# One large product a step ahead of the scores, value products of a pair in two runs, norm rows on VectorE: one change to a hybrid attention and mLSTM step

## The chip, the cores and the metric

The kernel runs on 1 core of one Trainium2 chip. The metric is device time in microseconds (us) from start to end of one execution. Engines are called by the profile's short names: PE (TensorE, matrix products; PEld its weight loads), ACT (ScalarE), DVE (VectorE), POOL (GpSimd) and SP (SyncE, which issues DMAs). Each engine takes its instructions strictly in the order in which the program lists them for it; a wait for another engine holds all that stands behind it.

## The reference, cut to what matters

One layer of a hybrid backbone: 128 context tokens and 1024 latent tokens of width 1024, so 9 blocks of 128 tokens (block 0 is the context). Grouped-query attention (8 query heads of 64, 2 key heads) and a bidirectional mLSTM run side by side; the output projection joins them, and a SwiGLU follows. All is float32.

```python
aq = apply_rope(rmsnorm(aq.reshape(B, T, N_Q_HEADS, HEAD_DIM), q_norm_w), *rope)
s = jnp.einsum('bqhgd,bkhd->bhgqk', qi, k).astype(F32) * ATTN_SCALE
p = jax.nn.softmax(s, axis=-1).astype(v.dtype)
o = jnp.einsum('bhgqk,bkhd->bqhgd', p, v)
...
mix = jnp.concatenate([attn_o, hm], axis=-1) @ w_out        # hm: the mLSTM's part
x = x + g1 * mix
h2 = rmsnorm(x, norm2_w) * (1 + sc2) + sh2
x = x + g2 * swiglu(h2, w_gu, w_down)
```

Each latent block of 128 queries has 1152 keys (1024 latent, 128 context), so a head's scores are 128 x 1152.

## The kernel before

Modulation, input projection, keys and the mLSTM come first; the gate, up and down products of the SwiGLU fill the second half of the span. Between them lies the stage that the change touches: attention over the 8 latent blocks, with the remaining query products, the output projection and the second norm woven in.

**Steps.** The stage is a Python loop over steps. Step n belongs to head n of 64 (block 1 + n // 8, head n % 8). Before the change a step writes, in this order: the scores of head n + 2 on PE (`head_scores`, six matmuls at L1110 into one of two score buffers, which the exponential of head n must have left); filler work on PE; in odd steps the value products of a pair of heads (18 matmuls at L1053, for the two heads n - 3 and n - 2); on DVE and ACT the normalised probabilities of head n as a float16 pair (`ph` at L1509, `pl` at L1517), each turned by a DMA transpose; the maximum (L1114) and the exponential (L1118) of head n + 1; the sums of the value products of the step before (ACT L1058 and L1059 into `ol`, POOL L1061); then filler work on ACT and DVE. One `ph` a step makes it the clock by which steps are counted.

**Fillers.** `Filler` holds tasks as generators. Each piece of a task names its engine, a cost, a lag in steps behind the piece before it, the PSUM banks it needs and a condition. `run` writes the pieces whose lag, bank and condition allow it as long as the engine's credit is above zero; the credit grows each step by PE 3.5, ACT 1.9, DVE 2.0 and is capped at one and a half of that. The pieces with lag 0 are written after the others. Names such as `turned` or `rope` are stamped with the step in which a piece was written. The tasks:

- `q_task(b)`, blocks 3 to 8: a query product in two halves (12 matmuls each, L1287 to L1289), copied to `q_rest` (ACT L726). The blocks go in pairs (3, 4), (5, 6), (7, 8); with the second of a pair comes its rope: a square on ACT (L663, into a scratch tile that the rope's products reuse), a sum and a small chain on DVE (L666; L125 to L131), then seven operations on POOL (L669, four of L680, L686, L687).
- `turn_task(b)`: four PE transposes of a block's roped queries (L114, `q_rest`), copies and splits into `qT`. It may start two steps after the rope is stamped, and for block 3 not ahead of step 9.
- `hm_task(b)`: the mLSTM's rows of a block are transposed and split (`ring`), and the output projection's lower half runs as two products of 12 matmuls (`out_block`, L1142 to L1144); the gated sum goes to the residual rows (DVE L1133, POOL L1136).
- `mix_task(b)`: the same for the attention's half when a block's heads are done (`kst`), then the second norm: sum of squares (ACT L1425), a reciprocal root (DVE L1189 to L1196), rows scaled by it (`norm_rows`, ACT L1432, twice 512 columns into two tiles `y`), eight PE transposes into two banks, scale and shift (ACT L1451, DVE L1453), and a float16 split (ACT L1461, POOL L135).
- `w_task`, `first_piece`: loads and splits of the out weights and of the first gate weights.

The last block's norm is done by `norm2`, beside the first gate products (L1180 to L1182).

Of the kernel before, what the change touches and what calls it, by code (L numbers as in the profile page):

```python
# [45 lines left out]
def hybrid_step(ctx: ExitStack, tc: tile.TileContext, I: dict, O: dict):  # L46
# [998 lines left out]
    def value_products(b, j, nk, kv, rhs):  # L1045
        if j == 0:
            oT[b] = new_oT(b)
        po = po2[:, n_po[0] % 2 * 256 : n_po[0] % 2 * 256 + 256]
        n_po[0] += 1
        for n in range(nk):  # L1050
            v = vs[:, NB if nk == 1 else n, kv].rearrange("p t d -> p (t d)")
            for t in range(2):
                mm(po, v, rhs(t, n), start=(n == 0 and t == 0), stop=(n == nk - 1 and t == 1))  # L1053
        return b, j, po
# [92 lines left out]
    def norm2(b, new=None):  # L1147
# [6 lines left out]
        for half in range(2):  # L1154
            y = fp.tile([P, 512], F32, name=nm("y"), tag="y", bufs=2)
            act(y, x1[b][:, half * 512 : (half + 1) * 512], AF.Copy, scale=rs[b])
            pss.append(y)
            yield 0.1
# [73 lines left out]
    class Filler:  # L1232

        def __init__(self, **per_step):
            self.per_step, self.credit = per_step, dict.fromkeys(per_step, 0.0)
            self.tasks, self.step, self.banks = [], 0, 2
# [9 lines left out]
        def run(self, engine, behind=False):  # L1246
            order = sorted((t for t in self.tasks if t[1][0] == engine), key=lambda t: t[1][1])
            for task in order:
                while task[1] is not None:
# [3 lines left out]
                    if not behind and self.credit.get(engine, 1.0) <= 0.0 or ready is not None and not ready():  # L1253
                        break
                    if engine in self.credit:
# [12 lines left out]
    fl = Filler(PE=3.5, ACT=1.9, DVE=2.0)  # L1268
# [8 lines left out]
    def q_task(b):  # L1277
# [18 lines left out]
        yield "ACT", 1.1, 0, 0, lambda: b - 2 < CB or ("rope", b - 2) in at  # L1296
# [88 lines left out]
    def mix_task(b):  # L1385
# [15 lines left out]
        yield "ACT", 1.35, 1, 0, lambda: b == 0 or ("turned", b - 1) in at  # L1401
# [26 lines left out]
    def norm_rows(b):  # L1428
        ys = []
        for half in range(2):  # L1430
            y = fp.tile([P, 512], F32, name=nm("y"), tag="y", bufs=2)
            act(y, x1[b][:, half * 512 : (half + 1) * 512], AF.Copy, scale=rs[b])  # L1432
            ys.append(y)
        return ys
# [55 lines left out]
    def step(n):  # L1490
# [3 lines left out]
        if n + 2 < len(heads):  # L1494
            head_scores(n + 2)
        fl.run("PE")
# [3 lines left out]
        elif n % 2 == 1 and (n - 3) // 2 in pairs:  # L1500
            m = (n - 3) // 2
            two = pairs.pop(m)
            now = [value_products(heads[2 * m][0], m % 4, NB, m % 4 // 2, lambda t, i: two[t][:, :, i, :])]
# [105 lines left out]
    pairs, late = {}, []  # L1609
    pieces = [Piece(0, lambda: wp.tile([P, 1024], F32, name=nm("braw"), tag="raw", bufs=2), ("whi", "wlo"))]  # L1610
    pieces += [Piece(f) for f in range(1, NF)]
    with tc.manual_schedule(engines=ENGINES):
# [22 lines left out]
        while n < len(heads) + 4 or fl.tasks:  # L1635
# [263 lines left out]
```

## Time and profile before

| | us |
|---|---|
| median of 3 runs | 1646.91 (1644.01 to 1648.23) |
| the profiled execution's own time | 1645.31 |
| its span, first to last instruction | 1643.5 |
| first score product starts | 435.1 |
| first gate product starts | 837.45 |

A row of the profile that shows an instruction has its start, its length, the engine, the line, the operation and what it writes and reads; brackets give the engine's idle time ahead of it and what ended it. A row for a group of instructions has the count, the busy time in us, the mean in ns, and the idle time ahead of the group with its main releasers. Tile names appear without their numbers. A PE row's length includes the pipeline, so the distance of starts is the better measure of a run of matmuls. The chain of work that ended last covers only the last part of this stage; the stage is therefore read by windows and waits.

### The profile page before, as it was taken

To read this page: it belongs to the slowest core of one execution; us is meant where nothing else is said; L and a number is where in the kernel's file an instruction comes from. 1 tells how busy PE (TensorE), PEld (TensorE's weight loads), DVE (VectorE), ACT (ScalarE), POOL (GpSimd) and SP (SyncE) were. 2 spreads that over 40 slices of the span, in tenths; PEclk is the share of its full clock that TensorE was granted. 3 is DMA by queue.
4 is the path that set the end of the run, shared out by engine and by line. 5 is a ranking of instruction groups with operands and counts; after the bars stand their busy time and mean duration, and the time that the engine had idled before them with its cause. 6 is when DMAs were issued, how large, how long until landed. Compare 5 with 4: busy or idle time off the path is not lost.

```text
span 1643.5 us, 22904 instructions
## 1 busy us (share of the span) xinstructions
PE 1489.5 (91%) x8651; PEld 921.1 (56%) x8651; DVE 902.0 (55%) x2160; ACT 732.4 (45%) x1428; POOL 251.1 (15%) x272
## 2 busy tenths in 40 slices
PE   5899999898596799877689989999999999999995
PEld 2755666575454677655455555456664466655542
DVE  3844355849765777877645456333353333442278
ACT  3744343345465666778655666003340032422023
POOL 0411021303224522333320000000000000000001
PEclk8899999999598899999799999999999999999998
DMA  9345462301285789556357553421104310120213
GB/s 353 114 142 150 93 144 62 73 1 19 60 174 99 149 190 193 101 102 127 72 180 252 184 194 100 140 93 52 52 27 141 115 52 28 50 77 14 83 59 116
DMA packets 281685, 181.83 MB, mean 111 GB/s; under 512 B 167302, under 2 KB 253782, under 8 KB 281574
## 3 DMA queue, kind: packets, MB, share of 16 engines
q1 hardware_dynamic: 280150, 177.96, 41.6%
q10 hardware_dynamic: 1424, 2.40, 0.4%
q8 instruction: 68, 1.11, 0.3%
q14 instruction: 43, 0.35, 0.1%
HBM read 122.71 MB, written 19.29 MB: 86 GB/s over the span
## 4 chain that ended last, share of the span: by engine, by line
PE 37%; DMA 5%; DVE 4%; ACT 4%; issue 1%; POOL 0%; ACTq 0%; SPq 0%; DVEq 0%; POOLq 0%
PE mm L1180 8%; PE mm L1182 8%; PE mm L1181 8%; PE mm L1751 4%; PE mm L1752 4%; PE mm L1753 4%; DMA wd_d<-wdt 3%; DMA wdt<-in_w_down_dram 2%; DVE x L1136 1%; ACT wdt L1546 1%; DVE wdt L1552 1%; ACT wdt L1551 1%; DVE t L1135 1%; ACT jk L1576 0%; ACT jk L1837 0%
## 5 line engine op out<-in xcount | busy, mean ns | idle before, releaser
L1180 PE MATMUL mm<-h,wpair 128*128 128x384 f16 x1056 | 345.0, 327 | 1.5 <-DVE fl L1453 1.5
L1181 PE MATMUL mm<-h,wpair 128*128 128x384 f16 x1056 | 345.0, 327 | 0.0
L1182 PE MATMUL mm<-h,wpair 128*128 128x384 f16 x1056 | 344.7, 327 | 0.0
L1714 DVE SCALAR_TENSOR_TENSOR tn<-tn,mm 128x384 f32<-128x384 f32 x66 | 36.4, 552 | 217.5 <-PE mm L1182 139.6
L1751 PE MATMUL mm<-wd,hl 128*128 128x512 f16 x396 | 149.9, 379 | 0.0
L1752 PE MATMUL mm<-wd,hl 128*128 128x512 f16 x396 | 149.9, 379 | 0.0
L1753 PE MATMUL mm<-wd,hl 128*128 128x512 f16 x396 | 149.6, 379 | 0.0
L1180 PEld LDWEIGHTS <-wpair 128*128 128x128 f16 x1056 | 105.4, 100 | 67.3 <-issue 0.7
L1182 PEld LDWEIGHTS <-wpair 128*128 128x128 f16 x1056 | 103.5, 98 | 68.7 <-issue 0.7
L1181 PEld LDWEIGHTS <-wpair 128*128 128x128 f16 x1056 | 103.5, 98 | 68.7 <-issue 2.3
L1110 PE MATMUL S<-kst,qT 128*128 128x512 f32 (+1 forms) x384 | 97.3, 394 | 47.9 <-ACT pr L1118 46.0
L499 PE MATMUL wi<-ipair,hT 128*128 128x384 f16 (+2 forms) x384 | 124.7, 325 | 2.8 <-ACT ipair L216 2.8
L1840 POOL TENSOR_TENSOR x<-x,fw 128x512 f32<-128x512 f32 x9 | 11.5, 1274 | 756.7 <-ACT jk L1837 756.7
L501 PE MATMUL wi<-ipair,hT 128*128 128x384 f16 (+2 forms) x384 | 124.4, 325 | 0.4 <-POOL hT L135 0.4
L500 PE MATMUL wi<-ipair,hT 128*128 128x384 f16 (+2 forms) x384 | 124.7, 325 | 0.0
L1717 ACT ACTIVATE jk<-tn 128x384 bf16<-128x384 f32 x66 | 34.4, 521 | 196.8 <-DVE tn L1715 145.1
L1576 ACT ACTIVATE jk<-braw 128x1024 bf16<-128x1024 f32 x44 | 45.9, 1044 | 152.9 <-DVE x L1136 152.1
L1517 DVE SCALAR_TENSOR_TENSOR pl<-pr,st,ph 128x1152 f16<-128x1152 f32 x64 | 95.1, 1486 | 31.9 <-ACT ph L1509 29.0
L1509 ACT ACTIVATE ph<-pr,st 128x1152 f16<-128x1152 f32 x64 | 80.3, 1254 | 68.0 <-issue 59.6
L1110 PEld LDWEIGHTS S<-kst,qT 128*128 128x128 f32 x384 | 69.9, 208 | 72.2 <-ACT pr L1118 58.6
L1114 DVE TENSOR_REDUCE st<-S 128x1 f32<-128x1152 f32 x64 | 86.7, 1355 | 39.9 <-PE S L1110 39.4
L1135 DVE SCALAR_TENSOR_TENSOR t<-mm,gm,gl 128x512 f32<-128x512 f32 x64 | 47.7, 745 | 81.3 <-PE mm L1753 81.3
(427 smaller groups left out, 2854.5 us busy)
## 6 DMA issues: line engine op xcount, KB each, us to landing
wd<-wd_d SPq DMA_DIRECT2D x58, 512.0 KB
braw<-in_w_gu_dram SPq DMA_DIRECT2D x44, 512.0 KB
a4s<-in_w_ada_dram SPq DMA_DIRECT2D x32, 512.0 KB
wdt<-in_w_down_dram SPq DMA_DIRECT2D x22, 512.0 KB
wd_d<-wdt SPq DMA_DIRECT2D x22, 512.0 KB
aw<-in_w_ada_dram SPq DMA_DIRECT2D x16, 512.0 KB
x<-in_x_sample_dram SPq DMA_DIRECT2D x16, 512.0 KB
iraw<-in_w_in_dram SPq DMA_DIRECT2D x32, 256.0 KB
```

The lines of the kernel that those rows point to most:

```text
L499: mm(ps[:, :n], ah, wh[:, k % 2, c0 : c0 + n], start=(k == 0), stop=False)
L500: mm(ps[:, :n], ah, wl[:, k % 2, c0 : c0 + n], start=False, stop=False)
L501: mm(ps[:, :n], al, wh[:, k % 2, c0 : c0 + n], start=False, stop=(k == KD - 1))
L1110: mm(S[:, lo:hi], qTs[b][:, h, :], kst[kv][:, t, lo:hi], start=(t == 0), stop=(t == 1))
L1114: dve.tensor_reduce(out=stat[n][:, 0:1], in_=score[n], axis=AX.X, op=ALU.max, negate=True)
L1180: mm(ps, wh[:, k, :], th[:, k, :], start=(k == 0), stop=False)
L1181: mm(ps, wh[:, k, :], tl[:, k, :], start=False, stop=False)
L1182: mm(ps, wl[:, k, :], th[:, k, :], start=False, stop=(k == KD - 1))
L1517: dve.scalar_tensor_tensor(out=pl, in0=pr, scalar=st[:, 3:4], in1=ph, op0=ALU.mult, op1=ALU.subtract)
L1751: mm(ps, ah, w[:, k, 0], start=(j + k == 0), stop=False)
L1752: mm(ps, ah, w[:, k, 1], start=False, stop=False)
L1753: mm(ps, al, w[:, k, 0], start=False, stop=(j + k == g["nf"] - 1))
```

## The change

Three things are done.

- **The order of a step on PE.** The filler pieces of a step now stand ahead of its scores. A piece of cost above 2.0 (a half of a query product or an out-projection product) is written at most once a step, and PE's credit grows by 3.3. The value products of a pair are cut in two: key blocks 0 to 4 (10 matmuls) behind the scores of the odd step, key blocks 5 to 8 (8 matmuls) at the head of the next step. Their sums are written a step later, and the loop has one step more at its end.
- **The rope.** The square of a pair's rope is written not as soon as the rope of the pair before it is stamped, but at least 3 steps after that.
- **The norm's rows.** `norm_rows` is one DVE operation of 128 x 1024 into one tile in place of two ACT operations of 128 x 512 into two, in the eight mixes and in `norm2`.

```diff
-    def value_products(b, j, nk, kv, rhs):
-        if j == 0:
+    def value_products(b, j, nk, kv, rhs, po=None, part=(0, NB)):
+        if j == 0 and po is None:
             oT[b] = new_oT(b)
-        po = po2[:, n_po[0] % 2 * 256 : n_po[0] % 2 * 256 + 256]
-        n_po[0] += 1
-        for n in range(nk):
+        if po is None:
+            po = po2[:, n_po[0] % 2 * 256 : n_po[0] % 2 * 256 + 256]
+            n_po[0] += 1
+        for n in range(nk)[slice(*part)]:
...
+                    if engine == "PE" and cost > 2.0:
+                        if self.big == self.step:
+                            break
+                        self.big = self.step
...
-    fl = Filler(PE=3.5, ACT=1.9, DVE=2.0)
+    fl = Filler(PE=3.3, ACT=1.9, DVE=2.0)
...
-        yield "ACT", 1.1, 0, 0, lambda: b - 2 < CB or ("rope", b - 2) in at
+        yield "ACT", 1.1, 0, 0, lambda: b - 2 < CB or since(("rope", b - 2), 3)
...
-        yield "ACT", 1.35, 1, 0, lambda: b == 0 or ("turned", b - 1) in at
+        yield "DVE", 0.75, 1, 0, lambda: b == 0 or ("turned", b - 1) in at
         ys = norm_rows(b)
...
     def norm_rows(b):
-        ys = []
-        for half in range(2):
-            y = fp.tile([P, 512], F32, name=nm("y"), tag="y", bufs=2)
-            act(y, x1[b][:, half * 512 : (half + 1) * 512], AF.Copy, scale=rs[b])
-            ys.append(y)
-        return ys
+        y = fp.tile([P, D], F32, name=nm("y"), tag="y", bufs=1)
+        dve.tensor_scalar(out=y, in0=x1[b], scalar1=rs[b], scalar2=None, op0=ALU.mult)
+        return [y[:, 0:512], y[:, 512:1024]]
...
-        if n + 2 < len(heads):
-            head_scores(n + 2)
-        fl.run("PE")
         now = []
         if n < 2:
             now = [value_products(*first_values[2 * n + i]) for i in range(2)]
-        elif n % 2 == 1 and (n - 3) // 2 in pairs:
+        elif n % 2 == 0 and half:
+            args, po = half.pop()
+            now = [value_products(*args, po, (5, NB))]
+        fl.run("PE")
+        if n + 2 < len(heads):
+            head_scores(n + 2)
+        if n % 2 == 1 and (n - 3) // 2 in pairs:
             m = (n - 3) // 2
             two = pairs.pop(m)
-            now = [value_products(heads[2 * m][0], m % 4, NB, m % 4 // 2, lambda t, i: two[t][:, :, i, :])]
+            args = (heads[2 * m][0], m % 4, NB, m % 4 // 2, lambda t, i: two[t][:, :, i, :])
+            half.append((args, value_products(*args, None, (0, 5))[2]))
...
-        while n < len(heads) + 4 or fl.tasks:
+        while n < len(heads) + 5 or fl.tasks:
```

In the changed program the lines from there on have other numbers: the scores' matmuls are L1111, the value products L1054, `ph` L1513, the query products L1290 to L1292, the out-projection products L1143 to L1145.

What this does to the order of instructions is shown at three places, with one row for each run of like matmuls. The first is PE in steps 8 and 9, where block 3's queries are transposed (`mm<-ident,q_rest`). Before, from the scores of head 10 on (`S2`, the score buffers; `ipair` and `hT2` make a query product, here both halves of block 7's):

```order
L1110 MATMUL S2_4796<-kst0_4270,qT_938_4856 128x128 x2
L1287 MATMUL mm_1015_5301<-ipair_790_4255,hT2_293 128x512
L1110 MATMUL S2_4796<-kst0_4270,qT_938_4856 128x512 x4
L114 MATMUL mm_1024_5342<-ident_79,q_rest_4274 128x128 x4
L1287 MATMUL mm_1015_5301<-ipair_792_4262,hT2_293 128x512
```

Now, from the value products ahead of the scores of head 10 on (the query product is block 6's):

```order
L1054 MATMUL po2_4797<-phT_978_5081,vs_4789 128x256
L1290 MATMUL mm_1013_5268<-ipair_790_4255,hT2_293 128x512
L1111 MATMUL S2_4796<-kst0_4270,qT_938_4856 128x128 x2
L114 MATMUL mm_1020_5301<-ident_79,q_rest_4274 128x128 x4
L1290 MATMUL mm_1013_5268<-ipair_792_4262,hT2_293 128x512
L1111 MATMUL S2_4796<-kst0_4270,qT_938_4856 128x512 x4
```

The transposes stood behind the scores of head 11 and stand ahead of them now, in the same step 9. The stamp of the first pair's rope moves from step 6 to step 7.

The second place is ACT around the square of the second pair's rope (`nr0`, L663). Before, from `ph` of head 7 on:

```order
L1509 ACTIVATE ph_1009_5277<-pr_999_5209,st_998_5207 128x1152
L1118 ACTIVATE pr_1012_5283,st_1011_5281<-S2_4796,st_1011_5281 128x1152
L726 ACTIVATE q_rest_4274<-mm_988_5136,vsc_88 128x512
L1372 CAST kst0_4270<-mm_1008_5252 128x512
L663 ACTIVATE nr0_1014_5293<-q_rest_4274 128x1024
L1509 ACTIVATE ph_1016_5316<-pr_1012_5283,st_1011_5281 128x1152
```

Now, from `ph` of head 10 on (`qT` is the copy of the transposes shown above):

```order
L1513 ACTIVATE ph_1026_5367<-pr_1024_5342,st_1023_5340 128x1152
L1119 ACTIVATE pr_1031_5375,st_1030_5373<-S2_4796,st_1030_5373 128x1152
L726 ACTIVATE q_rest_4274<-mm_1013_5268,vsc_88 128x512
L1314 CAST qT_1032_5380<-mm_1020_5301 64x4x128 x2
L663 ACTIVATE nr0_1033_5383<-q_rest_4274 128x1024
L1513 ACTIVATE ph_1036_5417<-pr_1031_5375,st_1030_5373 128x1152
```

The square stood in step 7, one step behind the first pair's rope, and stands in step 10, three steps behind it.

The third place is PE from step 20 on, where two out-projection products stood in one step (`wlo` the weights, `ring0` and `ring1` the rows of blocks 1 and 2). Before:

```order
L1142 MATMUL mm_1111_5864<-wlo_967_5012,ring0_5703 128x512
L1110 MATMUL S2_4796<-kst1_4271,qT_1041_5439 128x512 x4
L1142 MATMUL mm_1120_5906<-wlo_1001_5219,ring0_5703 128x512
L1142 MATMUL mm_1121_5919<-wlo_967_5012,ring1_5704 128x512
L1053 MATMUL po2_4797<-phT_1099_5793,vs_4789 128x256
L1110 MATMUL S2_4796<-kst0_4270,qT_1104_5807 128x128 x2
```

Now:

```order
L1143 MATMUL mm_1116_5874<-wlo_966_4999,ring0_5761 128x512
L1111 MATMUL S2_4796<-kst1_4271,qT_1032_5380 128x512 x4
L1054 MATMUL po2_4797<-phT_1097_5782,vs_4789 128x256
L1143 MATMUL mm_1124_5935<-wlo_1000_5194,ring0_5761 128x512
L1111 MATMUL S2_4796<-kst0_4270,qT_1101_5793 128x128 x2
L1143 MATMUL mm_1133_5977<-wlo_966_4999,ring1_5762 128x512
```

Each score product now has at most one such product on either side, and the value products stand directly behind the scores of the odd step. The first attention out-projection (block 0) is written at step 41 in place of 39, and the last piece of the stage at step 72 in place of 70.

More of the change, by code (lines that the diff above doesn't have):

```diff
@@ L1153, in norm2 @@
         pss = []
-        for half in range(2):
-            y = fp.tile([P, 512], F32, name=nm("y"), tag="y", bufs=2)
-            act(y, x1[b][:, half * 512 : (half + 1) * 512], AF.Copy, scale=rs[b])
-            pss.append(y)
-            yield 0.1
+        pss += norm_rows(b)
+        yield 0.1
+        yield 0.1
         for half, y in enumerate(pss):
@@ L1235, in __init__ @@
             self.per_step, self.credit = per_step, dict.fromkeys(per_step, 0.0)
-            self.tasks, self.step, self.banks = [], 0, 2
+            self.tasks, self.step, self.banks, self.big = [], 0, 2, -1
         def add(self, gen):
@@ L1428, in norm_rows @@
     def norm_rows(b):
-        ys = []
-        for half in range(2):
-            y = fp.tile([P, 512], F32, name=nm("y"), tag="y", bufs=2)
-            act(y, x1[b][:, half * 512 : (half + 1) * 512], AF.Copy, scale=rs[b])
-            ys.append(y)
-        return ys
+        y = fp.tile([P, D], F32, name=nm("y"), tag="y", bufs=1)
+        dve.tensor_scalar(out=y, in0=x1[b], scalar1=rs[b], scalar2=None, op0=ALU.mult)
+        return [y[:, 0:512], y[:, 512:1024]]
     def norm_turn(ys):
@@ L1606, in fold @@
             dve.tensor_scalar(out=v[:, 7:8], in0=v[:, 4:5], scalar1=v[:, 5:6], scalar2=wds[:, self.f, 3:4], op0=ALU.mult, op1=ALU.mult)
-    pairs, late = {}, []
+    pairs, late, half = {}, [], []
     pieces = [Piece(0, lambda: wp.tile([P, 1024], F32, name=nm("braw"), tag="raw", bufs=2), ("whi", "wlo"))]
```

## The prediction

> **What bounds the kernel now.** I read the busy shares of the page first, then the waits, then windows cut at the joints of the one stage that the change touches.
>
> ```profile
> PE 1489.5 (91%) x8651; PEld 921.1 (56%) x8651; DVE 902.0 (55%) x2160; ACT 732.4 (45%) x1428; POOL 251.1 (15%) x272
> ```
>
> Over the whole span TensorE (PE) is nearly full. The stage in which the scores run is another matter; its ends are the first score product and the first gate product:
>
> ```profile
> L1110 PE MATMUL S<-kst,qT x384: 221/395/795, 435.1 to 791.4; 128*128 128x512 f32 x128, 128*128 128x128 f32 x64
> 837.45 0.32 PE L1180 MATMUL mm<-h,wpair 128*128 128x384 f16 x1 [1.46 <-DVE fl L1453]
> 435.00:557.00 122.00, 95.32 (x462) 62.60 (x462) 80.78 (x132) 72.32 (x100) 46.53 (x43) 0.86 0.63 123
> 557.00:666.00 109.00, 99.82 (x544) 79.51 (x545) 85.70 (x118) 74.11 (x103) 34.01 (x42) 0.98 0.88 184
> 666.00:806.00 140.00, 108.05 (x576) 81.84 (x575) 110.12 (x216) 107.29 (x170) 51.31 (x57) 0.95 0.59 109
> 806.00:837.50 31.50, 21.06 (x93) 15.64 (x92) 9.49 (x26) 13.25 (x25) 12.42 (x13) 0.81 0.47 137
> ```
>
> Columns of a window: length, busy PE, weight loads, DVE (VectorE), ACT (ScalarE), POOL (GpSimd), clock. The stage lasts 402.4 us, 435.1 to 837.45. Only from 557 to 666 is PE the bound (99.8 of 109 us). Before that it stands idle 26.7 us; after 666 PE, DVE and ACT have 108, 110 and 107 of 140 us, none full, so there they wait for one another. Nothing behind 837.45 changes apart from one row scaling, which lies beside a full PE, so the forecast is a forecast of when that first gate product starts.
>
> ```profile
> PE S L1110 <- ACT pr L1118: 46.0, 27, 8.3
> DVE t L1133 <- PE mm L1144: 20.5, 12, 5.6
> ACT nr L663 <- POOL q_rest L687: 7.8, 1, 7.8
> ```
>
> The waits (total, times, longest): PE stood 46.0 us ahead of score products, because the score buffer is free only when the exponential of the head two earlier is done. In the old order that wait comes ahead of the filler products; the new order puts fillers there.
>
> ```profile
> 443.04 1.25 ACT L1509 ACTIVATE ph<-pr,st 128x1152 f16<-128x1152 f32 x1 [0.48 <-DVE st L1507]
> 805.93 1.25 ACT L1509 ACTIVATE ph<-pr,st 128x1152 f16<-128x1152 f32 x1 [1.09 <-issue]
> ```
>
> One `ph` stands for one step. 64 of them, the first and last shown: (805.93 - 443.04) / 63 = 5.76 us a step.
>
> **The change part by part.**
>
> *(a) The rope of the second pair is held three steps.* ScalarE's square (L663) stood at step 7; its scratch tile is still being read by GpSimd's rope of the first pair.
>
> ```profile
> 486.10 1.90 POOL L669 TENSOR_TENSOR q_rest<-q_rest,ry 128x1024 f32<-128x1024 f32 x1 [1.00 <-POOL oT L1061]
> 495.36 2.34 POOL L687 TENSOR_TENSOR q_rest<-q_rest,nr 128x1024 f32<-128x1024 f32 x1
> 486.31 1.26 ACT L1509 ACTIVATE ph<-pr,st 128x1152 f16<-128x1152 f32 x1 [0.74 <-ACT wlo L1327]
> 497.73 1.06 ACT L663 ACTIVATE nr<-q_rest 128x1024 f32<-128x1024 f32 x1 [7.83 <-POOL q_rest L687]
> 498.69 1.24 ACT L1509 ACTIVATE ph<-pr,st 128x1152 f16<-128x1152 f32 x1
> 501.18 2.07 PE L1110 MATMUL S<-kst,qT 128*128 128x512 f32 x4 [8.26 <-ACT pr L1118]
> ```
>
> GpSimd is busy 486.10 to 497.70 (11.6 us), ScalarE idles 7.83 us, the step lasts 12.38 us, PE idles 8.26. At step 10, two ordinary steps after the rope's start at the end of step 7 (2 x 5.76 = 11.5), the tile is free just in time. Against an ordinary step: 12.38 - 5.76 = **-6.6 us**. Bounds: 0 if another wait stands there, -8.3 if all of PE's idle time goes.
>
> *(b) A wait in its place.* One large product a step puts the second half of block 4's query product at step 4 instead of 3, so the first pair's rope starts at the end of step 7 instead of 6. But the transposes of block 3, which read what that rope writes, stay at step 9, and since fillers now stand ahead of the step's scores, they are one place earlier among the score products (between those of heads 10 and 11, no longer behind 11). PE issues in order: behind those transposes wait a query product and the scores of head 11, and for these the exponential of head 11.
>
> ```profile
> 482.99 0.17 DVE L125 TENSOR_SCALAR rv<-nrs 128x16 f32<-128x16 f32 x1
> 485.79 0.18 DVE L131 SCALAR_TENSOR_TENSOR ry<-rt,ry 128x16 f32<-128x16 f32 x1
> ```
> ```profile
> 490.16 0.39 PE L1287 MATMUL mm<-ipair,hT 128*128 128x512 f16 x1
> 492.54 0.38 PE L1289 MATMUL mm<-ipair,hT 128*128 128x512 f16 x1
> 585.94 1.42 PE L1110 MATMUL S<-kst,qT 128*128 128x128 f32 x6 [0.81 <-ACT pr L1118]
> 587.20 0.60 PE L114 MATMUL mm<-ident,t 128*128 128x128 f32 x4
> L1114 DVE TENSOR_REDUCE st<-S 128x1 f32<-128x1152 f32 x64 | 86.7, 1355 | 39.9 <-PE S L1110 39.4
> L1118 ACT ACTIVATE pr<-S,st 128x1152 f32<-128x1152 f32 x64 | 78.0, 1219 | 25.7 <-DVE st L1114 25.0
> L1118 ACT ACTIVATION_READ_ACCUMULATOR pr<-S,st 128x1 f32 x64 | 12.3, 193 | 0.0
> L1507 DVE TENSOR_SCALAR st<-st 128x1 f32<-128x1 f32 x64 | 9.8, 154 | 2.2
> L1517 DVE SCALAR_TENSOR_TENSOR pl<-pr,st,ph 128x1152 f16<-128x1152 f32 x64 | 95.1, 1486 | 31.9 <-ACT ph L1509 29.0 <-DMA plT<-pl 1.2
> L135 DVE TENSOR_TENSOR ring<-mm,ring 128x512 fp32r<-128x512 f32 x8 | 5.5, 682 | 0.0
> L135 DVE TENSOR_TENSOR whi<-raw,whi 128x1024 fp32r<-128x1024 f32 x2 | 2.5, 1258 | 0.0
> ```
>
> The rope's small chain on VectorE (first and last of 12 shown, 2.98 us) ends just ahead of `ph` of step 8; GpSimd is done some 11.3 us after that. Then follow four transposes (0.6), a query product (first and last of its 12 matmuls: 2.76), six score matmuls (1.42), the maximum (1.36), the exponential (1.22 and 0.19 for its sum) and two small operations (0.3): 19.2 us from `ph` 8 to `ph` 11, against 3 x 5.76 = 17.3. That is +1.9. VectorE's step 7 now holds this chain beside a ring split (0.7) and a weight split (1.3): with two small operations, the maximum and `pl` 0.3 + 1.4 + 1.5 + 0.7 + 1.3 + 3.0 = 8.2, that is +2.4 over an ordinary step. And PE will have stood still for over 8 us:
>
> ```profile
> 815.61 0.80 PE L1142 MATMUL mm<-wlo,kst 128*128 128x512 f32 x1 [4.67 <-DVE fl L1453]
> 820.90 0.44 PE L1053 MATMUL po<-phT,vs 128*128 128x256 f16 x1
> ```
>
> After a gap of 4.67 us a product of 12 took 5.29 us (815.61 to 820.90), nearly twice 2.76: +2.5. Together **+6.8 us**; bounds 0 (the rope is done in time, or its wait lies beside other work) and +8.5 (the scores at half speed too).
>
> *(c) Fewer products ahead of that point.* Up to the scores of head 10 PE now carries two query products less (2 x 2.76 = 5.5). If PE is the bound between steps 2 and 6, they bring the steps forward by all of it; if VectorE's 8.2 us is, by nothing. I take half: **-2.7 us**. The two products come back in steps 11 to 17, inside the 26.7 us of PE's idle time in the first window; if that cover is gone they cost 5.5.
>
> *(d) The middle.* In steps 21, 29 and 37 two out-projection products and a pair's value products stood in a row, and PE idled after the first two of these:
>
> ```profile
> 626.17 1.41 PE L1110 MATMUL S<-kst,qT 128*128 128x128 f32 x6 [0.81 <-ACT pr L1118]
> ```
>
> The other is the row at 585.94, 0.81 as well. Both go: **-1.6 us**; bounds -9.2 (all of PE's idle time in that window) and 0. The split of the value products itself moves nothing: 10 and then 8 matmuls follow each other on PE as the 18 did. Their sums come a step later; no one waits for them but the out-projection of a block, which is queued behind other blocks until the end.
>
> *(e) The late stretch.* Eight norm-row scalings leave ScalarE and come to VectorE.
>
> ```profile
> L1432 ACT ACTIVATE y<-x,r 128x512 f32<-128x512 f32 x16 | 10.6, 710 | 2.3 <-DVE r L1196 2.3
> L340 DVE TENSOR_SCALAR x<-x,ry x9: 745/749/755, 9.0 to 57.8; 128x1024 f32<-128x1024 f32 x9
> L1133 DVE TENSOR_TENSOR t<-mm,gl 128x512 f32<-128x512 f32 x32 | 21.9, 686 | 17.9 <-PE mm L1144 17.8
> ```
>
> ScalarE loses 10.6 us, VectorE gains 8 x 0.75 = 6.0 (the same shape at L340). If both bound alike, -4.6. Against this stands the order: the residual addition waits less for its product, but the scores now wait for it. Per product the loop through PE has the scores (1.42) where the loop through VectorE had the addition and two small operations (0.69 + 0.3): +0.4, over 16 products +6.9 if PE holds the loop each time; I count half. -4.6 + 3.4 = **-1.2 us**; bounds -10.6 and +8.3.
>
> ```profile
> 784.70 1.29 POOL L1136 TENSOR_TENSOR x<-x,t 128x512 f32<-128x512 f32 x1 [0.24 <-DVE fv L1584]
> 784.72 1.29 DVE L1585 TENSOR_SCALAR fv<-fv 128x2 int32<-128x2 int32 x1
> 786.05 0.17 DVE L1586 TENSOR_SCALAR fv<-fv 128x2 int32<-128x2 int32 x1
> ```
>
> These rows say that a VectorE operation of a few elements can last as long as a GpSimd operation that began just before it (1.29 us both): the next of the same size took 0.17. If that befalls a row scaling, it costs up to 1.3 us; GpSimd is busy 51.3 of 140 us here, so 8 x 0.37 x 0.65 = 1.9 us of VectorE's idle time, and I add nothing. [...]
>
> *(f) The end.* The loop runs two steps longer (73, not 71). Behind the last `ph` (805.93) PE must now also do an out-projection product (2.76) and a block's transposes. Before, PE stood idle in that part 31.5 - 21.1 = 10.4 us, 4.67 of it for a bank that the norm of blocks 5 and 6 held; that norm stands there as before, so most of the addition lies beside it: **+1.5 us**, bounds 0 and +5.3 (a product at half speed).
>
> DMA: the loads of the out weights, the latent rows and the first gate weights are issued one or two steps later on SyncE's queue, each still two steps or more ahead of its use; costed at nothing, and a load that came late would cost PE its wait. The transposes to value tiles keep their places; the value products of a pair now stand ahead of a filler, so one product (2.76) less covers their landing.
>
> **Sum.** The profiled execution took 1645.3 us (span 1643.5 and 1.8 around it); the median of the three runs is 1646.9, 0.1% above. -6.6 + 6.8 - 2.7 - 1.6 - 1.2 + 1.5 = -3.8, so 1645.3 - 3.8 = 1641.5, rounded to **1642 us**.
>
> **Rivals.**
>
> 1. *The rope wait does not bite* ((b) at 0): -10.6, about 1635. For it: the scores of heads 9 and 10 are ready, so ScalarE and VectorE run on for two steps. Against it: PE is in order and GpSimd's 11.6 us are twice those two steps.
> 2. *Most waits ahead of scores close.* Of 46.0 us, 8.3 belong to (a). Half of the rest is 19, with (a) and (b) cancelling: about 1625. Against it: those waits are for exponentials, and these wait in turn for VectorE and ScalarE, each 75% full.
> 3. *Slower: scores held behind a product that is held.* A filler now stands ahead of the scores, and its input is often made on ScalarE and VectorE in the step just before (the copies of the eight mixes, the rows of eight norms: 16 places). The old order covered that wait with the scores (1.42). If in each place the input is done later than the exponential that frees the score buffer, the scores of the next head slip by 0.9 us on average (between the 0.4 above and 1.42): 16 x 0.9 = +14.4, about 1656. It decides where PE's gap stands ahead of a product or a transpose and no longer ahead of scores.
> 4. *The scaling is locked out by GpSimd at every block*: 8 x 1.29 = +10.3, about 1652. The rows above bear it out for a small operation only. [...]
> 5. *The change gives back what it takes* ((b) at its upper bound, (c) at 0): about 1646.
>
> That the change does not do what it says is excluded by the order of instructions: no step holds two large products any more.
>
> **How the numbers follow.** Forecast 0.45, rivals 0.16, 0.10, 0.18, 0.06, 0.05. A measurement of this kernel tells 0.3% (4.9 us) from no change, so faster means below 1640.4 and slower above 1650.2. The forecast (1636 to 1650) lies below that line with 0.12, above it with 0.02 and within with 0.31. Faster: 0.12 + 0.16 + 0.10 = 0.38. Slower: 0.02 + 0.18 + 0.04 of rival 4 = 0.24. Same: 0.31 + 0.05 + 0.02 = 0.38. The range, 1628 to 1656, leaves out rival 2 and half of rival 3. Cases of both signs hold much: the forecast's own range is 1636 to 1650.
>
> **What would show it.** (a) the wait of L663 for L687 gone, `ph` 7 to `ph` 8 near 8 us. (b) a PE gap of 8 us or more ahead of the transposes of block 3, released by GpSimd, with a lower clock after it; if there is none, rival 1. (d) no 0.81 gaps ahead of scores in steps 21 to 40. (e) ScalarE's row scaling gone, VectorE's at 0.75 (at 2 us, rival 4); `t` waiting less than 17.8 us. Rival 3 by PE gaps ahead of L1142's and the rows' transposes above 20 us in all. (f) last `ph` to first gate product 31 to 34 us. The forecast is wrong if the steps 18 to 63 change by more than 10 us, which (d) and (e) do not provide for.

## The result and the profile after

| kernel | median, us | ratio to before, 95% interval |
|---|---|---|
| before (4 runs) | 1645.46 | 1 |
| changed (4 runs) | 1825.72 (1822.36 to 1830.32) | 1.1099 [1.1062, 1.1137] |

The change made the kernel 180 us slower; the prediction was 1642. The profiled execution's span grew by 182.8 us (1826.3 against 1643.5). First the page's busy line and the windows of the changed kernel, columns as before:

```profile
PE 1551.1 (85%) x8651; PEld 962.5 (53%) x8651; DVE 905.4 (50%) x2169; ACT 722.3 (40%) x1410; POOL 248.0 (14%) x272
437.00:561.00 124.00, 80.46 (x345) 47.16 (x346) 61.11 (x99) 56.44 (x78) 22.12 (x26) 0.79 0.48 98
561.00:785.00 224.00, 151.01 (x666) 116.05 (x665) 103.63 (x150) 92.12 (x127) 54.67 (x58) 0.84 0.49 104
785.00:989.00 204.00, 131.56 (x563) 101.15 (x563) 108.21 (x208) 94.87 (x149) 48.02 (x53) 0.78 0.39 72
989.00:1023.40 34.40, 22.42 (x99) 16.44 (x99) 16.65 (x41) 14.26 (x27) 16.47 (x17) 0.85 0.42 123
```

All of the loss lies in the attention stage: 437.1 to 1023.35, 586 us where it was 402. VectorE and ScalarE are busy about as long as before (290 and 258 us in the stage, before 286 and 267). TensorE's instructions take 385.5 us instead of 324.3 (+61, at a granted clock of 0.78 to 0.85), and the rest of the window, in which it does nothing, grew from 78 to 201 us (+123). The long stretch in the middle is the plainest: before, the granted clock was 0.98 in the second window and PE was busy for 99.8 of its 109 us; now no window is near full on any engine. The waits:

```profile
DVE st L1115 <- PE S L1111: 265.6, 56, 12.3
ACT pr L1119 <- DVE st L1115: 239.2, 55, 12.4
PE po L1054 <- ACT ol L1060: 89.0, 32, 6.3
PE mm L1143 <- DVE t L1134: 17.4, 5, 5.5
PE mm L1143 <- DVE st L1510: 17.0, 5, 4.1
PE S L1111 <- ACT pr L1119: 14.8, 9, 2.8
PE mm L114 <- POOL q_rest L687: 8.2, 1, 8.2
```

VectorE's maximum now waits 265.6 us for score products (39.4 before), the exponential nearly as long for the maximum, and the value products, which had not waited for them before, 89.0 us for ScalarE's sums. TensorE's wait ahead of scores fell, as hoped, from 46.0 to 14.8. Two steps in order of time, from the middle window:

```profile
632.74 1.26 PE L1111 MATMUL S<-kst,qT 128*128 128x512 f32 x6
634.04 1.36 DVE L1115 TENSOR_REDUCE st<-S 128x1 f32<-128x1152 f32 x1 [5.38 <-PE S L1111]
637.43 0.15 DVE L1511 TENSOR_SCALAR st<-st 128x1 f32<-128x1 f32 x1
637.77 0.27 PE L1054 MATMUL po<-phT,vs 128*128 128x256 f16 x1 [2.66 <-ACT ol L1060]
638.87 0.78 PE L1143 MATMUL mm<-wlo,ring 128*128 128x512 f32 x1
643.00 1.32 PE L1111 MATMUL S<-kst,qT 128*128 128x128 f32 x6
644.36 1.36 DVE L1115 TENSOR_REDUCE st<-S 128x1 f32<-128x1152 f32 x1 [6.78 <-PE S L1111]
645.63 1.41 DVE L1521 SCALAR_TENSOR_TENSOR pl<-pr,st,ph 128x1152 f16<-128x1152 f32 x1
645.75 1.22 ACT L1119 ACTIVATE pr<-S,st 128x1152 f32<-128x1152 f32 x1 [6.41 <-DVE st L1115]
646.96 0.68 DVE L135 TENSOR_TENSOR ring<-mm,ring 128x512 fp32r<-128x512 f32 x1
647.79 0.63 PE L114 MATMUL mm<-ident,q_rest 128*128 128x128 f32 x4 [3.47 <-DVE ring L135]
```

By the order of a step, the maximum at 644.36 is that of head n + 1: its own scores are the six products at 632.74, done by 634.04. VectorE is free from 637.58 and stands still for 6.78 us, until the scores of head n + 2 (643.00) end. Ahead of those stand the second run of value products, which waited 2.66 us, and a whole out-projection product. And VectorE's part of the filler (`ring`, 646.96) stands behind that maximum and `pl`, so TensorE then waits 3.47 us for it; in both traces all of VectorE's instructions (2160 before, 2169 now) start in the order in which the built program lists them. So the engines take turns.

**Why a maximum waits for another head's scores.** The two score buffers are column ranges of one tile, S2 (0 to 1151 for odd heads, 1408 to 2559 for even ones). An instruction is recorded when the Python program calls it, so all engines' instructions stand in one order of recording, whatever the order in which they run; from it the build works out who waits for whom. In the built programs of before and after alike, the maximum of an even head waits for the product that writes columns 1024 to 1151, the last one of the odd head (all 32 do), and the maximum of an odd head for that at column 2048 (31 do): the last product into the tile that was recorded ahead of the reader, whatever its columns. Before, those scores stood first in the step, so the wait was short. The same holds for `po2`, one tile with two halves for the value products: in the changed program 32 of these wait for a sum that reads the half they do not write. I call this theory G, the guard of the tile. The guard is a set of waits in the built program, put there when the kernel is built.

### The profile page after: what moved, and what is told of

Read it like the earlier page. It is cut to its first block, busy times and chain, and to the rows that moved or that the text cites. A ratio compares the mean times of both kernels' runs of the same rounds, so it can differ in the third digit from the quotient of the medians.

```text
span 1826.3 us, 22856 instructions
## 1 busy us (share of the span) xinstructions
PE 1551.1 (85%) x8651; PEld 962.5 (53%) x8651; DVE 905.4 (50%) x2169; ACT 722.3 (40%) x1410; POOL 248.0 (14%) x272
## 5 line engine op out<-in xcount | busy, mean ns | idle before, releaser
L1115 DVE TENSOR_REDUCE st<-S 128x1 f32<-128x1152 f32 x64 | 86.9, 1357 | 265.6 <-PE S L1111 265.6
L1119 ACT ACTIVATE pr<-S,st 128x1152 f32<-128x1152 f32 x64 | 78.1, 1220 | 239.2 <-DVE st L1115 239.2
L1054 PE MATMUL po<-phT,vs 128*128 128x256 f16 x292 | 81.8, 311 | 94.3 <-ACT ol L1060 89.0
L1054 PEld LDWEIGHTS <-vs 128*128 128x128 f16 x584 | 61.4, 110 | 113.7 <-issue 102.1
L1721 ACT ACTIVATE jk<-tn 128x384 bf16<-128x384 f32 x66 | 34.4, 522 | 203.0 <-DVE tn L1719 151.8
L1111 PE MATMUL S<-kst,qT 128*128 128x512 f32 (+1 forms) x384 | 100.5, 404 | 16.5 <-ACT pr L1119 14.8
L1844 POOL TENSOR_TENSOR x<-x,fw 128x512 f32<-128x512 f32 x9 | 11.5, 1275 | 753.0 <-ACT jk L1841 753.0
L1513 ACT ACTIVATE ph<-pr,st 128x1152 f16<-128x1152 f32 x64 | 80.3, 1254 | 57.2 <-issue 51.0
```

The source lines that it names most:

```text
L1111: mm(S[:, lo:hi], qTs[b][:, h, :], kst[kv][:, t, lo:hi], start=(t == 0), stop=(t == 1))
L1115: dve.tensor_reduce(out=stat[n][:, 0:1], in_=score[n], axis=AX.X, op=ALU.max, negate=True)
```

## The experiments

The first four were made with two theories: B, that the second run of a pair's value products waits for the sums of the pair before; and S, that filling work ahead of the scores holds them back.

### First four: which edit

**e1_whole**: the changed kernel, value products of a pair in one run again.

> The changed kernel with the value products of a pair whole again (18 matmuls behind the scores of the odd step, sums one step later); all else as changed. Theory B (bank): the second run of value products waits for the sums of the pair before, because the program guards the two halves of one PSUM bank as one; those sums now stand between the two runs. Then this run is back at 1635 to 1655 us and PE waits under 5 us for L1060 ahead of the value products. Theory S (scores): fillers ahead of the scores hold them back; then it stays above 1780 us.

**e2_split_alone**: before, with the cut in two runs only.

> The kernel before with the cut of the value products alone (10 matmuls at the end of the odd step, 8 at the head of the next, sums a step later); scores first, two products a step allowed, rows on ScalarE. Theory B: the wait for the sums appears here too, 1720 to 1800 us. Theory S: about 1646 us, within 10.

**e3_sums_now**: the changed kernel, the sums in the step of the second run.

```diff
-        for v in late:
+        for v in now:
             value_sums(*v)
-        late[:] = now
...
```

> The changed kernel with the sums of a pair written in the step of its second run of value products, not one step later; the cut stays. Theory B: the sums then stand ahead of the next pair's first run by a step, the wait goes, 1635 to 1655 us. Theory S: stays above 1780 us.

**e4_scores_first**: the changed kernel, the scores again ahead of the filling work.

```diff
+        if n + 2 < len(heads):
+            head_scores(n + 2)
         fl.run("PE")
-        if n + 2 < len(heads):
-            head_scores(n + 2)
```

> The changed kernel with the fillers of a step behind its scores again; cut, one large product a step, rope and rows as changed. Theory B: still 1740 us or more, with PE waiting 60 us or more for L1060. Theory S: 1640 to 1660 us.

Measured (each ratio is to runs of the kernel before that were taken beside the version): e1 1789.94 us, ratio 1.0879 [1.0822, 1.0936]; e2 1677.34, 1.0195 [1.0128, 1.0262]; e3 1783.42, 1.084 [1.079, 1.089]; e4 1672.91, 1.0168 [1.0112, 1.0224]. e1 and e3 came out as S said, e2 and e4 as neither said; neither theory stands alone. The cut costs some 30 us, and putting the sums a step earlier (e3) gives back 42 of the change's 180. The order of scores and filling work is the larger part: undoing it (e4) gives back 153.

### e6_fill_first_alone and e7_rest_alone: do the parts add up

e6 is before with `fl.run("PE")` moved ahead of `head_scores(n + 2)`; e7 is the changed kernel without that order and without the cut.

> The kernel of before with one edit, the filling work ahead of the scores of head n+2 instead of behind them; no cut of the value products, up to 3.5 us of products a step, rope and norm rows as before. If the order of scores and products is the whole of the loss (both theories on the maximum), 1755 to 1800 us. If the loss needs the limit of one large product a step or the cut as well, under 1700 us. VectorE's idle time that ends with scores rises from 39 us to over 180 us in the first case.

> The changed kernel with scores ahead of the filling work again and with the value products whole, so that what is left is the limit of one large product a step, the rope that is held three steps, and the norm rows on VectorE. By the terms of the prediction for these (rope of the second pair -6.6 us, middle -1.6, norm rows -1.2, end +1.5, with the new wait of +6.8 only where scores stand behind the turn) 1635 to 1645 us; by the theory that the limit itself starves the steps, 1665 us or more.

e6: 1783.34 us, 1.0847 [1.0819, 1.0875], inside its first range. e7: 1654.22, 1.0069 [1.0042, 1.0095], slower than the prediction's terms and faster than the rival. Order, cut (e2) and the rest are 8.5 + 1.9 + 0.7 = 11.1%, and the change measured 11.0%. The waits of e6:

```profile
DVE st L1114 <- PE S L1110: 214.5, 58, 9.1
ACT pr L1118 <- DVE st L1114: 180.4, 54, 8.8
```

### e5_max_first and e11_max_exp_first: the same instructions, other waits

Both start from e3. e5 records the maximum of head n + 1 ahead of TensorE's part of the step; e11 also the conversion and the exponential (the last three of the added lines are in e11 alone; all are taken away further down in the step; the lines that fetch the tiles are left out here).

```diff
...
+            dve.reciprocal(st[:, 2:3], st[:, 1:2])
+            dve.tensor_scalar(out=st[:, 3:4], in0=st[:, 2:3], scalar1=2.0 ** 14, scalar2=None, op0=ALU.mult)
+            if n + 1 < len(heads):
+                head_max(n + 1)
...
+            act(ph, pr, AF.Copy, scale=st[:, 3:4])
+            if n + 1 < len(heads):
+                head_exp(n + 1)
         now = []
...
         fl.run("PE")
         if n + 2 < len(heads):
             head_scores(n + 2)
```

The sequences of TensorE, GpSimd and SyncE are the same in e3, e5 and e11. On VectorE three of 2169 instructions stand elsewhere, behind the attention stage, and ScalarE's order differs only from the gate products on. What changes is whom the readers of S2 wait for: in e5 and e11 the maximum waits for its own last product (column 2048 for an even head).

> The changed kernel with its sums in the step of the second run (1783.4 us in an earlier run), and VectorE's maximum of head n+1 recorded ahead of TensorE's work of step n instead of behind it; VectorE's own order stays as it was, and so does TensorE's. Theory G (guard of the tile): both heads' scores are slices of one tile, and the program makes a reader of the tile wait for the last product that was recorded into the tile ahead of it, which is that of the other head; with the maximum recorded first it waits for its own scores alone, and the large product ahead of the scores of n+2 has nothing left to hold. Then 1625 to 1665 us, and VectorE's idle time that ends with scores falls from 219 us to under 60 us in the scores. Theory H (the scores are held because the large product ahead of them waits for its bank and for VectorE's copies): the order of recording is nothing, and the time stays at 1760 to 1790 us with some 200 us of such idle time.

> The kernel with the maximum recorded first (1697.1 us in an earlier run), and the exponential of head n+1 recorded ahead of TensorE's part as well, with the conversion that stands ahead of it on ScalarE; no engine's own order changes. In the earlier run ScalarE's exponentials waited 117.7 us in all for the scores of the other head. Theory G expects that wait to fall under 25 us and the time to 1640 to 1670 us. The rival (what is left of the loss is the cut of the value products, +32 us by itself, and the price of the scores' late start) expects 1685 to 1700 us.

e5: 1697.06 us, 1.0325 [1.0302, 1.0347], outside both expectations: 86 us went, where theory G's range asked for 118 at least. Its waits say where the rest was:

```profile
ACT pr L1119 <- PE S L1111: 117.7, 55, 11.7
```

The exponential reads the tile too, was still recorded behind the other head's scores, and took the maximum's place as the one held. e11 takes that away as well: **1646.52 us, 1.001 [0.9991, 1.0029]**. With the change's order, cut, limit, rope and rows all in place, and the sums in the step of the second run, the loss is gone. Rows of e11 from the same part of the stage, and its waits:

```profile
628.25 1.31 PE L1111 MATMUL S<-kst,qT 128*128 128x128 f32 x6
629.60 1.36 DVE L1115 TENSOR_REDUCE st<-S 128x1 f32<-128x1152 f32 x1
630.99 1.22 ACT L1119 ACTIVATE pr<-S,st 128x1152 f32<-128x1152 f32 x1 [0.18 <-DVE st L1115]
632.36 1.37 PE L1111 MATMUL S<-kst,qT 128*128 128x512 f32 x6 [1.92 <-ACT pr L1119]
PE S L1111 <- ACT pr L1119: 37.2, 25, 2.8
DVE st L1115 <- PE S L1111: 35.8, 28, 8.9
437.00:832.40 395.40, 323.58 (x1670) 243.35 (x1671) 292.50 (x497) 257.94 (x379) 148.00 (x152) 0.90 0.69 138
```

The maximum now follows its own scores at once. The guard has only turned round: the scores at 632.36 wait for the exponential of the other head (1.92 us). Such waits come to 37.2 us in all, less than the 46.0 that TensorE stood ahead of scores before the change. TensorE's busy time in the stage is back at 323.6 us.

### e8_no_shared_bank: the tile or the bank

The kernel lays S2 out as five banks of 512 columns (`5 * 512`), and the two heads share the third (columns 1024 to 1535). e8 is e3 with the products into that bank left out from the third head on.

```diff
         for lo, hi in zip(cuts, cuts[1:]):
+            if n > 1 and hi - lo == P:
+                continue
```

> The changed kernel with its sums in the step of the second run, with the 128 columns of scores that share a bank with the other head's computed for the first two heads alone: from the third head on those score products are left out (a ninth of the scores), and the maxima read stale columns there. Theory G (the guard covers the whole tile, whatever bank): VectorE's maximum still waits for the other head's products, and the time stays within 25 us of 1783 us less the work left out (124 products of 64 x 128 columns, some 10 to 20 us): 1745 to 1785 us. Theory K (readers and writers of one bank lock each other out): no bank is shared any more, 1630 to 1680 us.

1770.85 us, 1.0775 [1.0738, 1.0811]: G. In the built program the maximum of an even head now waits for the odd head's product at column 512 (31 of the 32 do), in a bank it does not read.

```profile
DVE st L1117 <- PE S L1113: 208.7, 51, 14.1
```

So the slow order does not come from the shared bank. For `po2`, whose two halves together are 512 columns wide, no run tells the tile from the bank.

### e17_cut_sums_now: the cut's price

e2 with the sums written from `now`, as in e3.

> The kernel of before with the value products of a pair in two runs, and with the sums of a pair in the step of its second run instead of a step later. The cut alone took 1677.3 us, with 53 us of TensorE's idle time ahead of the second run ending with ScalarE's sums of the pair before. Theory G (the wait is one on the other half of the tile, and goes when those sums are recorded a step earlier): 1640 to 1655 us, and under 10 us of such idle time. The rival (the two runs themselves cost it): 1665 to 1680 us.

1642.5 us, 0.9996 [0.998, 1.0012], against 1677.34 for the cut with its sums a step later: theory G's range. Wait of e2, which e17 no longer has:

```profile
PE po L1054 <- ACT ol L1060: 52.9, 31, 3.3
```

The cut costs nothing by itself; its 32 us were the wait of the second run, into one half of `po2`, for the sums that read the other half.

### e10_before_max_first and e18_max_ahead: the guard in the old order

e10's new lines ended up behind `head_scores(n + 2)`, since in the old step those stand ahead of `now = []`. e18 does it right, on top of the rows on VectorE: the maximum stands at the head of the step, ahead of the scores and of the reciprocal.

```diff
+        if n + 1 < len(heads):
+            head_max(n + 1)
         if n + 2 < len(heads):
             head_scores(n + 2)
...
-                head_max(n + 1)
                 head_exp(n + 1)
```

> The kernel of before with VectorE's maximum of head n+1 recorded ahead of TensorE's part of step n; no engine's own order changes. The guard of the tile then turns round: the maximum no longer waits for the scores of n+2, which stand first in the step, but these scores wait for that maximum, though they write other columns. Theory G expects VectorE's idle time ending with scores to fall from 39 us to under 10 us, and TensorE's wait ahead of the scores to move from the exponential to VectorE's maximum; the sum of both is open by it, 1630 to 1665 us. The rival (no guard of the tile; each waits only for its own columns) expects 1640 to 1650 us and the same waits as before.

> The kernel of before with the norm rows on VectorE (1641.6 us in an earlier run), and with VectorE's maximum of head n+1 moved to the start of step n: it is recorded ahead of the scores of n+2 and stands ahead of the reciprocal of head n on VectorE. By theory G the maximum then waits for its own scores alone and runs beside the exponential of head n; the exponential of n+1 still waits for the scores of n+2, so a turn of the loop is scores and exponential, some 2.9 us, where it was scores, maximum and exponential, some 4.2 us. If that loop sets the pace in the shorter steps, 1615 to 1637 us; if the filling work does, as the 5.8 us of a mean step say, 1637 to 1645 us.

e10: 1644.57 us, 1.0004 [0.9991, 1.0017]. The maxima wait for the same products as before, so it tells nothing of the theories. e18: **1722.97 us, 1.0474 [1.045, 1.0499]**, a clear miss of mine, 78 us above the upper of the two ranges. Waits and rows of e18:

```profile
PE S L1110 <- DVE st L1114: 101.6, 42, 6.5
648.78 0.69 DVE L1133 TENSOR_TENSOR t<-mm,gl 128x512 f32<-128x512 f32 x1 [1.72 <-PE mm L1144]
649.38 1.35 DVE L1114 TENSOR_REDUCE st<-S 128x1 f32<-128x1152 f32 x1
650.79 1.84 PE L1110 MATMUL S<-kst,qT 128*128 128x512 f32 x6 [2.12 <-DVE st L1114]
652.66 1.22 ACT L1118 ACTIVATE pr<-S,st 128x1152 f32<-128x1152 f32 x1 [0.33 <-PE S L1110]
```

I had foreseen that the maximum no longer waits. That the scores of n + 2 then wait for it stood in the expectation for e10 and was left out of the one for e18. They write other columns, but it is now the tile's last recorded reader, and on VectorE it stands behind the residual addition (648.78), which waits for TensorE's product. So product, addition, maximum and scores form one chain. It is the guard again, seen from the writer's side.

### e12, e13, e14: the three small edits alone

Each is before with one part of the change's diff: rows on VectorE (e12), the limit of one large product and PE=3.3 (e13), `since(("rope", b - 2), 3)` (e14).

> The kernel of before with one edit: the norm rows scaled by one VectorE instruction of 1024 elements, with the task due to VectorE. The prediction's terms give -1.2 us for this with its cost to the products' copies in it; rival 4 (VectorE locked out by GpSimd's work) +5 to +12. So 1642 to 1647 us, or 1650 to 1658 us.

> The kernel of before with one edit: at most one large product a step, and 3.3 instead of 3.5 us of products a step. The three edits without the cut and the order were slower by 8.7 us (4 to 13). If the limit is the cause (products are left for later steps, so the turn of the last blocks and the end come later), 1650 to 1660 us; if it is the held rope or the norm rows, 1640 to 1648 us.

> The kernel of before with one edit: the rope tasks of the later blocks are held back three steps behind the rope that they follow. The prediction gave -6.6 us for this (a rope on GpSimd no longer queued with what TensorE waits for), so about 1638 us. By what the other edits alone gave (limit +6, rows -2, all three +9), the hold is worth +5 us: 1648 to 1652 us.

e12: 1641.58 us, 0.9987 [0.9975, 1.0]. e13: 1650.38, 1.0035 [1.0015, 1.0056]. e14: 1645.15, 1.0005 [0.9991, 1.002]. e13 came at the edge of the range for a cost of the limit; e14 lies outside both its figures, and e12 just below its lower range. Together +0.27%, where e7 had 0.69 [0.42, 0.95]; with their intervals these agree. In e13 the 64 heads are done sooner (first to last `ph` 359.2 us, before 362.9), but from the last `ph` to the first gate product it takes 40.5 us in place of 31.5: the products put off come at the end.

### e15, e16, e19: is the order itself slow

All three have the readers recorded first as e11, and neither limit nor held rope. e15 keeps the cut; e16 has the value products whole, their sums in the same step; e19 whole, sums a step later.

> The changed kernel with sums in the step of the second run and with maximum, conversion and exponential recorded first (1646.5 us in an earlier run), without the limit of one large product a step (3.5 us of products a step again) and without the held rope; the cut, the scores behind the filling work and the norm rows on VectorE stay. If the limit costs here what it cost alone (+6 us), 1638 to 1644 us. If the limit is what keeps scores behind at most one product from being late, and so earns its price in this order, 1648 to 1665 us.

> As the kernel without limit and hold, and with the value products of a pair in one run again; so what is left of the change is the order (filling work ahead of the scores), the sums in the step of the products, and the norm rows on VectorE, with the three readers recorded first. If the order alone is worth something once its waits are gone, 1625 to 1640 us; if it is worth nothing, 1640 to 1648 us. If the cut earns something here, this one is slower than the kernel that keeps it by over 3 us.

> The kernel with the filling work ahead of the scores, whole value products, norm rows on VectorE, no limit and no hold, with the three readers recorded first, and now with the sums of a pair a step behind its products, as before (with the sums in the step of the products it took 1724.3 us). If the order by itself is free once the tile's waits are gone, 1636 to 1652 us; if the scores' late start has a price of its own that the cut and the limit had paid, 1655 to 1710 us.

e15: 1659.3 us, 1.0091 [1.0072, 1.011]. e19: 1658.34, 1.0092 [1.0073, 1.0111]. Both lie in their second, slower range. e16: 1724.33, 1.0485 [1.0464, 1.0506], which none of my theories had; its trace shows ScalarE's sums waiting for the 18 products written in the same step, with the exponentials queued behind them:

```profile
ACT ol L1059 <- PE po L1054: 149.7, 33, 7.6
```

e19, which differs in the sums alone, is 66 us faster. So in this order the cut is worth nothing (e15 against e19), and the order without the limit is slow by 0.9% even without the guard's long waits. With the limit and the hold it is level (e11, 1.001), and the hold alone was worth nothing; so the limit, which costs 0.35% in the old order, seems to earn some 0.8% in the new one, likely by keeping the late scores behind one product at most. This is argued and not shown: the limit was not added to e15 by itself.

## Why the prediction was wrong, point by point

- **What bounds.** It read the 46.0 us of TensorE's wait rightly (14.8 after), but took the two score buffers as independent. The row of L1114 with 39.4 us `<-PE S` stood in the prediction and was passed over: a maximum whose scores were done a step before has nothing to wait for. That row was the guard.
- **(e) and rival 3, the step that failed.** The price of filling work ahead of scores was put at 0.4 us in 16 places, in the rival at 0.9 us in 16 places (+14.4, chance 0.18). It is 139 us (e6), 2.2 us a step over 64 steps. Rival 3 had the right sign and the right kind (scores behind a product), and its mark came too (17.4 and 17.0 us of gaps ahead of L1143, where it asked for over 20), but it let a late score hold only its own head; by the guard it holds the maximum and the exponential of the head before, which are due at once.
- **(d), "the split of the value products itself moves nothing".** Wrong: +32 us (e2), through the later sums and the guard of `po2`, and nothing at all without that (e17). That the sums come a step later was seen; the remark that no one but the out-projection waits for them was the error. The -1.6 us could not be seen under the rest.
- **(a) and (b)**, -6.6 and +6.8. The new wait for GpSimd came (8.2 us in the changed kernel) and L663 no longer waits. But the prediction booked a gain of the hold and a price of the limit, and each edit alone brings both: the hold (e14) shortens the first eight steps by 7.4 us and lengthens the next four by 7.4, the limit (e13) by 9.1 and 9.7. It is one trade, net near 0, as the sum of the two terms said.
- **(c)** and **(f)**, -2.7 and +1.5: of the limit. It measures +6 us alone (e13), with 9 us more at the end of the stage and 4 less in the heads. The changed kernel had 34.4 us there, just above the 31 to 34 foreseen.
- **(e), the rows themselves**: -1.2 with the copies' cost, e12 -2.1 us (0 to -4.1). Right in size; ScalarE's relief is not worth its 10.6 us.
- **Rival 4** did not come: the nine scalings (minimum, median, maximum in ns; e12, then the changed kernel) take the 0.75 us of the prediction, but for one of 1.09 us. The test was thin: of the nine of the changed kernel that one alone began while a GpSimd operation ran (998.60 to 999.87, the scaling at 999.33). There also one GpSimd addition (L1137) began early in a scaling (1018.46, the scaling at 1018.29), and it took 1.72 us, where the median is 1.28. Why these two took longer was not shown.

```profile
L1428 DVE TENSOR_SCALAR y<-x,r x9: 742/748/753, 684.2 to 837.9; 128x1024 f32<-128x1024 f32 x9
```
```profile
L1433 DVE TENSOR_SCALAR y<-x,r x9: 742/747/1090, 832.8 to 1026.1; 128x1024 f32<-128x1024 f32 x9
```

- **The range**, 1628 to 1656, missed by 170 us: no case in it had a wait in nearly every step (56 of 64 maxima wait). The last sentence of the prediction held: it was to be wrong if steps 18 to 63 changed by over 10 us, and from `ph` 18 to `ph` 63 they took 395.0 us instead of 249.3.
- **Readings that its rows do not give.** Rival 1 calls GpSimd's 11.6 us twice two steps, but two steps of 5.76 are 11.5. Rival 2 has VectorE and ScalarE 75% full; over the stage they were 71% and 66%. The upper bound of (e), +8.3, is not a sum of its terms (VectorE's 6.0 and the 6.9 give 12.9). None of these enters the forecast.

## What to carry to other kernels

Before moving work in a loop with double buffers, look at what each reader waits for in the built program, not at what it needs: buffers that are slices of one tile were one object to the guard here, and the order in which readers and writers were recorded decided who waits, with the engines' sequences in the stage unchanged (1783.42 us in e3, 1646.52 in e11). A short wait in the profile for something that should be long done was the sign of it (39.4 us in all before the change), and its price was set by what stood ahead of the thing waited for (265.6 us with products ahead of the scores). No version here beats the kernel of before by more than 0.13% (the rows on VectorE alone), and the interval of that one reaches 1.

## What the runs showed that was not expected

- Recording three readers earlier, with TensorE's whole sequence kept, is worth 137 us (e3 to e11); one reader moved ahead in the old order costs 81 us (e12 to e18).
- A third of the loss is the clock: TensorE's instructions in the stage took 61 of the 184 us more, at a granted clock of 0.81, before 0.92. Rows of the changed kernel after an idle time of TensorE:

```profile
662.33 0.77 PE L1143 MATMUL mm<-wlo,ring 128*128 128x512 f32 x1 [3.47 <-DVE st L1510]
662.89 0.63 PE L1144 MATMUL mm<-wlo,ring 128*128 128x512 f32 x1
663.32 0.63 PE L1145 MATMUL mm<-wlo,ring 128*128 128x512 f32 x1
665.74 0.40 PE L1145 MATMUL mm<-wlo,ring 128*128 128x512 f32 x1
665.97 0.39 PE L1143 MATMUL mm<-wlo,ring 128*128 128x512 f32 x1
```

  After 3.47 us of idleness the products start every 0.43 us, at a granted clock of 0.50 (662.33 to 665.40), and some 3 us later every 0.23, at 1.00 (665.74 to 667.60). Not every gap is followed by this. The first three rows here are of the changed kernel, the last two of e2:

```profile
655.07 0.27 PE L1054 MATMUL po<-phT,vs 128*128 128x256 f16 x1 [2.31 <-ACT ol L1060]
655.67 0.42 PE L1054 MATMUL po<-phT,vs 128*128 128x256 f16 x1
655.89 0.42 PE L1054 MATMUL po<-plT,vs 128*128 128x256 f16 x1
654.38 0.27 PE L1054 MATMUL po<-phT,vs 128*128 128x256 f16 x1 [2.22 <-ACT ol L1060]
654.60 0.27 PE L1054 MATMUL po<-phT,vs 128*128 128x256 f16 x1
```

  In the changed kernel a gap of 2.31 us was enough: within 0.6 us of the restart the value products start every 0.22 us, at a granted clock of 0.50 (655.46 to 658.00). In e2 they keep 0.11 us (every other one is shown) after a gap of 2.22. In the changed kernel itself two gaps of 2.66 us ahead of value products end differently: after the one up to 591.28 all eight keep 0.11 us (granted clock 1.00), after the one up to 709.62 they start every 0.21 from the fourth on (0.50 from 709.95). So the length of one gap alone does not settle it here, and what does was not tested. Nor is the price of idle time the same everywhere: in the changed kernel 123 us more of it came with 61 us of slower products, at a granted clock of 0.920 over the profiled run, before 0.958; e2, 32 us slower than before, had 0.961 and 0.954 in its two runs.
